# A decoder trunk whose float32 products are split in two: every fourth low part by an adding DMA

## The chip, the cores and the metric

The kernel runs on one core of one Trainium2 chip. The metric is the device time of one execution in microseconds (us); the time before is the median of two runs. A second record, the profile, comes from one further execution under the hardware profiler.

## The reference

Two decoder layers work on x, 256 tokens by 2048 features, in float32. Layer 0 mixes tokens by causal pooling (a product with `pool_w_in`, four trailing-window means, a 512 by 512 product for each of four channel groups, a product with `pool_w_out`). Layer 1 is dilated sliding-window attention with 24 heads of 128 (`attn_w_qkv` is 2048 by 9216, `attn_w_out` 1024 by 2048). After each mixer comes x = LN(alpha * x + mixer(x)), and then x = LN(alpha * x + relu(x @ w_up) ** 2 @ w_down) with 8192 hidden features. Nearly all arithmetic is products of 256 rows with large weights, each of which is read once.

## The kernel before

**Products in three terms.** TensorE gets operands of type float32r, which hold fewer bits than float32. Each float32 operand is therefore split: the high part is the value rounded to float32r, the low part is what is left. A product is summed up from high*high, low*high and high*low. For activations and weights alike, `split_from` (L61) does this: ScalarE copies the source into the high tile (L62), VectorE subtracts the high tile from the source into the low tile (L63).

**Weights in chunks.** `plan` and its helpers (L76 to L103) list all weights in the order of use as 744 chunks of 128 partitions by 1024 elements, 512 KB each: 2 blocks of 512 columns, or 4 blocks of 256. Counted from 0, chunk k passes through three steps, each with its own buffers. `load` (L108) starts a DMA on SyncE's queue into one of 4 `raw` buffers. `prefetch` (L117) splits a raw chunk into one of 8 `wh` and one of 8 `wl` buffers. TensorE then reads both. A raw buffer is free for the next load when its split is done; a `wh` or `wl` buffer is free when TensorE has done its last product with the chunk before in it.

**Order.** The instructions of TensorE, VectorE and ScalarE stay in the order in which the program writes them; the DMA queues and GpSimd are ordered by the framework's scheduler. `weights` (L128), called for each chunk in turn, first writes the splits of up to 8 chunks, the one about to be used among them, and returns that one. In the first pass over `pool_w_in` the number ahead is smaller: `min(2 + kc // 4, SPLITS)` (L183), where kc counts blocks of 128 rows, two to a chunk. `resident` (L134) takes several chunks that are used once for each of the two token tiles; the closing product of a sublayer (`closing`, L360) and the opening product of the next (`opening`, L422) work so, in order that the norm of one token tile runs beside products of the other. In `opening` only two chunks beyond the resident ones are split (L433) ahead of the second tile's products; the rest of the lookahead is written after them.

**What shares the queues with the splits.** On ScalarE: the copies of the second half of each product (L216), relu and square (L517, L519), the high parts of the activations. On VectorE: the sums and low parts that follow these, the residual sums (L277, L279, L555), the norms, and the postponed restoring of the residual (`restore`, L335), one block of 512 columns at the end of each of the next passes. On GpSimd: its few masks and counters, and the small loads of norm vectors (`gb`, L332; `last`, L512), some of which wait for a restore.

**Passes.** A pass of `feature_major` (L174) over 512 columns uses 8 chunks, each with 8 pairs of products: 512 columns with the high part (L189), 256 with the low part (L190). A pass of `token_major` (L234) uses 8 chunks too (L231).

Of the kernel before, what the change touches and what calls it, by code (L numbers as in the profile page):

```python
# [12 lines left out]
AF = mybir.ActivationFunctionType  # L13
OP = mybir.AluOpType
# [12 lines left out]
BACK = 128  # L27
# [5 lines left out]
MASKED = -1e30  # L33
CHUNK = 1024
RAWS = 4
SPLITS = 8
RESIDENT = 4
MLP_PARTS = 4
UP_FIRST = (256, 256, 512, 512, 512)
# [7 lines left out]
def trunk(ctx: ExitStack, tc: tile.TileContext, x, pool_w_in, pool_w_group, pool_scale, pool_w_out,  # L47
          attn_w_qkv, attn_w_out, mlp_w_up, mlp_w_down, ln_mix_g, ln_mix_b, ln_mlp_g, ln_mlp_b, out):
    nc = tc.nc
# [17 lines left out]

# [1 line left out]
    w_in, w_out = by_rows(pool_w_in[0]), by_rows(pool_w_out[0])  # L69
# [38 lines left out]
    def load(upto):  # L108
        """Start the loads of the chunks before `upto`."""
        while state["raw"] < min(upto, len(chunks)):  # L110
            src, step, ncols = chunks[state["raw"]]
            raw = wraw.tile([P, step, ncols], F32, tag="raw", name="raw")
            nc.sync.dma_start(raw, src)
            raws.append(raw)
            state["raw"] += 1

    def prefetch(upto):  # L117
        """Load and split the chunks before `upto`."""
        while state["split"] < min(upto, len(chunks)):
            load(state["split"] + 1)  # L120
            _, step, ncols = chunks[state["split"]]
            hi = wsplit.tile([P, step, ncols], F32R, tag="wh", name="wh")
            lo = wsplit.tile([P, step, ncols], F32R, tag="wl", name="wl")
            split_from(hi, lo, raws.pop(0))
            ready.append((hi, lo))
            state["split"] += 1

    def weights(ahead=SPLITS):  # L128
        """The next chunk, with those after it that fit into the buffers on their way."""
        prefetch(state["used"] + max(ahead, 1))  # L130
        state["used"] += 1
        return ready.pop(0)

    def resident(n):  # L134
        """The next n chunks, to be used more than once."""
        prefetch(state["used"] + n)
        state["used"] += n
        return [ready.pop(0) for _ in range(n)]

# [1 line left out]
    xz = const.tile([P, NT, D], F32, name="xz")  # L141
# [9 lines left out]

    # Per-feature vectors with the features on partitions: [128, 16] columns of each.
    rows = const.tile([7 * KT, P], F32, name="rows")
# [9 lines left out]

    # The transposed activations, the high and the low part of a block side by side.
    xT = const.tile([P, KT, 2, S], F32R, name="xT")
# [6 lines left out]

# [1 line left out]
    def feature_major(nk, ncols, act, start_up=None):  # L174
        """w.T @ act for the next pass, features on partitions: a bank for each block of 128 features,
        with the products of act's high part in its first half, those of its low part in the second."""
        nb = ncols // P
        kstep = CHUNK // ncols
        ps = [bank([P, 2, S], "pf") for _ in range(nb)]
        for kc in range(0, nk, kstep):  # L180
            if start_up is not None:
                start_up(kc)
            hi, lo = weights(SPLITS if start_up is None else min(2 + kc // 4, SPLITS))  # L183
            for j in range(kstep):
                k = kc + j
                a = act(k)
                for b in range(nb):
                    sl = slice(b * P, (b + 1) * P)
                    nc.tensor.matmul(ps[b], hi[:, j, sl], a, start=(k == 0), stop=False, skip_group_check=True)  # L189
                    nc.tensor.matmul(ps[b][:, 0, :], lo[:, j, sl], a[:, 0, :], start=False, stop=(k == nk - 1),  # L190
                                     skip_group_check=True)
        return ps

    def feature_pairs(nk, ncols, act):
        """The same with two blocks to a bank, the products of both parts of act added up."""
        nb = ncols // P
        kstep = CHUNK // ncols
        ps = [bank([P, 2, S], "pf") for _ in range(nb // 2)]
        for kc in range(0, nk, kstep):
            hi, lo = weights()  # L200
            for j in range(kstep):
                k = kc + j
                a = act(k)
                for b in range(nb):
                    sl = slice(b * P, (b + 1) * P)
                    for i, (w, part) in enumerate(((hi, 0), (hi, 1), (lo, 0))):
                        nc.tensor.matmul(ps[b // 2][:, b % 2, :], w[:, j, sl], a[:, part, :],  # L207
                                         start=(k == 0 and i == 0 and b % 2 == 0),
                                         stop=(k == nk - 1 and i == 2), skip_group_check=True)
        return ps  # L210

    def joined(out, ps):
        """The halves of each bank added up."""
        for b, p in enumerate(ps):
            low = tmp.tile([P, S], F32, tag="low", name="low")
            nc.scalar.activation(low, p[:, 1, :], AF.Copy)  # L216
            nc.vector.tensor_add(out[:, b, :], p[:, 0, :], low)  # L217
# [16 lines left out]
    def token_major(nk, ncols, act, shared=False, before_last=None):  # L234
        """Outputs [128 tokens, ncols] of both token tiles, in a bank of their own or in a shared one."""
        kstep = CHUNK // ncols
# [14 lines left out]
    def tile_products(ps, t, nk, parts, act, start=True, between=()):  # L251
        """The same for one token tile, from resident chunks."""
        k = 0
# [9 lines left out]

# [1 line left out]
    class Norm:  # L265
# [22 lines left out]
        def rstd(self, t, between=((), (), ())):  # L288
            r = self.r[t]
            nc.vector.reciprocal(r[:, 1:2], r[:, 0:1])  # L290
            self.centre(t, between[0])
            # One Newton step: r * (1.5 - 0.5 * v * r * r).
            nc.vector.tensor_scalar(r[:, 2:3], r[:, 4:5], r[:, 1:2], r[:, 1:2], op0=OP.mult, op1=OP.mult)
# [15 lines left out]
        def scaled(self, t, n):  # L309
            """Four transposed blocks, scaled and shifted per feature."""  # L310
            v = tmp.tile([P, 4, P], F32, tag="xv", name="xv", bufs=3)
# [13 lines left out]
        def restores(self):  # L325
            """The residual x = g * zhat + b, to be computed when the engines have time."""
            gbs = {}
# [32 lines left out]
    def closing(nk, act, first, norm, before_last=None):  # L360
        """The last product of a sublayer with its residual, the norm, and its transpose of token tile 0."""
        held = RESIDENT if norm.last is None else SPLITS
# [59 lines left out]
    def opening(norm, ncols):  # L422
        """The first product with the normed x, a token tile at a time, while the norm of tile 1 ends."""
        both = bank([P, NT, ncols], "pt")
# [12 lines left out]

# [1 line left out]
    def x_features(kc):  # L439
        """The blocks kc and kc + 1 of x, transposed and split."""  # L440
        pt = bank([P, 2, S], "ptr")
# [13 lines left out]
    with ExitStack() as ph:  # L455
        pool0 = ph.enter_context(tc.tile_pool(name="pool0", bufs=1))
        pbuf = ph.enter_context(tc.tile_pool(name="pbuf", bufs=2))
        # The pooled features; each group is then replaced by its product.
        pT = pool0.tile([P, KT, 2, S], F32R, name="pT")
# [46 lines left out]
    def mlp(norm_in, norm):  # L506
        with ExitStack() as ph:
# [6 lines left out]
            def hidden(ps):  # L514
                """relu(.) ** 2."""
                r = hb.tile([P, 2, S], F32, tag="r", name="r")
# [46 lines left out]

# [1 line left out]
    norm2 = Norm(ln_mix_g[1], ln_mix_b[1], 4)  # L565
    with ExitStack() as ph:
        ap1 = ph.enter_context(tc.tile_pool(name="ap1", bufs=1))
        ap = ph.enter_context(tc.tile_pool(name="ap", bufs=2))
        # dist[t][g][q, s] = s - q where query q of tile t sees key s in that group, else MASKED.
        dist = [ap1.tile([P, GROUPS, P * (t + 1)], F32, name=f"dist{t}") for t in range(NT)]  # L570
# [8 lines left out]
        def distances():  # L579
            for t in range(NT):  # L580
# [5 lines left out]
                for g, dil in enumerate(DILATIONS):  # L586
# [6 lines left out]
                    elif W > BACK:  # L593
                        # q - s <= BACK
                        nc.gpsimd.affine_select(out=dst, in_=dst, compare_op=OP.is_ge, fill=MASKED,
                                                base=BACK - t * P, pattern=[[1, W]], channel_multiplier=-1)
                    # s <= q
                    nc.gpsimd.affine_select(out=dst, in_=dst, compare_op=OP.is_ge, fill=MASKED,
# [19 lines left out]
        def scores(j, g, q, k, sc):  # L618
            """Scores of a head, biased and masked, into sc[t][:, g, :]."""
            b = j % 2  # L620
# [11 lines left out]
        def softmax(sc):  # L632
            """One softmax over the keys of all three groups."""
            ms = []
# [109 lines left out]
```

## Time and profile before

| what | value |
|---|---|
| median of 2 runs | 2161.73 us (2161.68 to 2161.79) |
| span of the profiled execution, first to last instruction | 2159.9 us |
| TensorE matmul busy | 2141.0 us, 99% |
| VectorE busy | 1284.2 us, 59% |
| ScalarE busy | 1058.4 us, 49% |
| GpSimd busy | 23.0 us, 1% |
| DMA | 404.69 MB, mean 187 GB/s |

The profiled execution has no time of its own beside its span; the median of the runs is 1.8 us above that span, which is what lies around the first and last instruction. Busy times of different engines overlap; the share that matters is that of the engine on which the end waits. The granted TensorE clock is full over nearly the whole span (mean 0.998).

### The profile page before, as it was taken

How to read it: one execution, taken by the hardware profiler on the slowest of the kernel's cores; microseconds unless marked ns; L12 is line 12 of the kernel's file. 1: busy time of each engine (PE TensorE's matmuls, PEld its weight loads, DVE VectorE, ACT ScalarE, POOL GpSimd, SP SyncE). 2: the span in 40 equal slices, each digit the busy share in tenths (PEclk: the TensorE clock that was granted, in tenths of full speed). 3: DMA queues.
4: the chain of work that ended last, by engine and by line, in shares of the span. 5: the costliest groups of instructions: out<-in, count | busy, mean ns of one | idle time of the engine just before them, and what ended most of it. 6: DMA issues, size and time to landing. Idle time of an engine off the chain costs nothing.

```text
span 2159.9 us, 30318 instructions
## 1 busy us (share of the span) xinstructions
PE 2141.0 (99%) x12033; PEld 1867.7 (86%) x12033; DVE 1284.2 (59%) x1558; ACT 1058.4 (49%) x1368; POOL 23.0 (1%) x52
## 2 busy tenths in 40 slices
PE   8999999999999999999999999999999999999998
PEld 7889888888888888898999898988888888888887
DVE  6785756555455555578656565676655555554555
ACT  4463654454355355354545444455545534644541
POOL 1000000000000000001000000000000000000000
PEclk9999999999999999999999999999999999999999
DMA  7565567665655655548554555456675565565552
GB/s 240 201 213 177 176 195 237 176 201 194 190 181 195 195 174 198 194 139 232 175 176 156 176 159 173 160 167 214 204 223 177 199 195 186 176 205 185 182 201 95
DMA packets 255662, 404.69 MB, mean 187 GB/s; under 512 B 12720, under 2 KB 109600, under 8 KB 255264
## 3 DMA queue, kind: packets, MB, share of 16 engines
q1 hardware_dynamic: 253088, 394.31, 55.9%
q0 software_dynamic: 2432, 8.45, 1.9%
q8 instruction: 94, 1.54, 0.3%
q14 instruction: 48, 0.39, 0.1%
HBM read 400.61 MB, written 2.10 MB: 186 GB/s over the span
## 4 chain that ended last, share of the span: by engine, by line
PE 97%; DVE 2%; DMA 1%; ACT 0%; issue 0%; SPq 0%; DVEq 0%; ACTq 0%
PE pt L231 45%; PE pf L189 32%; PE pf L190 16%; PE pf L207 1%; PE po L665 1%; PE pq L626 1%; DMA raw<-in_attn_w_qkv 0%; DVE wl L63 0%; PE ptr L307 0%; DMA raw<-in_pool_w_in 0%; ACT xv L316 0%; ACT wh L62 0%; DVE xT L323 0%; DVE xT L322 0%; DVE xz L349 0%
## 5 line engine op out<-in xcount | busy, mean ns | idle before, releaser
L63 DVE TENSOR_TENSOR wl<-raw,wh 128x1024 fp32r<-128x1024 f32 x744 | 898.4, 1224 | 643.3 <-ACT wh L62 638.9
L62 ACT ACTIVATE wh<-raw 128x1024 fp32r<-128x1024 f32 x744 | 775.9, 1058 | 823.1 <-PE pt L231 362.9
L189 PE MATMUL pf<-xT,wh 128*128 128x512 f32 x3008 | 1066.2, 399 | 0.0
L190 PE MATMUL pf<-xT,wl 128*128 128x256 f32 x3008 | 845.2, 281 | 0.3 <-DVE wl L63 0.3
L189 PEld LDWEIGHTS pf<-xT,wh 128*128 128x128 f32 x3008 | 566.1, 188 | 139.5
L190 PEld LDWEIGHTS pf<-xT,wl 128*128 128x128 f32 x3008 | 568.9, 189 | 1.1 <-DVE wl L63 0.8
L231 PE MATMUL pt<-wh,hH 128*128 128x512 f32 (+1 forms) x1088 | 406.7, 377 | 0.0
L231 PE MATMUL pt<-wl,hH 128*128 128x512 f32 (+1 forms) x1088 | 406.6, 377 | 0.0
L231 PE MATMUL pt<-wh,hL 128*128 128x512 f32 (+1 forms) x1088 | 397.9, 377 | 0.0
L231 PEld LDWEIGHTS pt<-wh,hH 128*128 128x128 f32 x1088 | 204.8, 188 | 37.6
L231 PEld LDWEIGHTS pt<-wl,hH 128*128 128x128 f32 x1088 | 204.8, 188 | 37.3
L231 PEld LDWEIGHTS pt<-wh,hL 128*128 128x128 f32 x1088 | 199.6, 188 | 37.4
L231 PE MATMUL pt<-wh,xT 128*128 128x256 f32 x896 | 167.0, 285 | 1.9 <-DVE xT L322 1.5
L231 PEld LDWEIGHTS pt<-wh,xT 128*128 128x128 f32 x896 | 141.4, 192 | 3.3 <-DVE xT L322 3.1
L231 PE MATMUL pt<-wl,xT 128*128 128x256 f32 x448 | 123.6, 283 | 0.0
L63 DVE TENSOR_TENSOR hL<-q,hH 128x512 fp32r<-128x512 f32 x62 | 42.9, 693 | 125.6 <-ACT hH L62 125.6
L216 ACT ACTIVATE low<-pf 128x256 f32<-128x256 f32 x188 | 64.7, 379 | 56.1 <-PE pf L190 49.1
L231 PEld LDWEIGHTS pt<-wl,xT 128*128 128x128 f32 x448 | 85.9, 192 | 0.0
L231 PE MATMUL pt<-wh,pT 128*128 128x512 f32 (+1 forms) x320 | 82.6, 347 | 0.0
L217 DVE TENSOR_TENSOR u<-pf,low 128x256 f32<-128x256 f32 x172 | 65.6, 420 | 13.0 <-ACT low L216 13.0
L517 ACT ACTIVATE r<-u 128x512 f32<-128x512 f32 x62 | 39.2, 632 | 49.6 <-DVE u L217 49.6
L231 PEld LDWEIGHTS pt<-wh,pT 128*128 128x128 f32 x320 | 56.1, 189 | 7.5
(126 smaller groups left out, 1000.8 us busy)
## 6 DMA issues: line engine op xcount, KB each, us to landing
raw<-in_mlp_w_up SPq DMA_DIRECT2D x256, 512.0 KB, 4.2
raw<-in_mlp_w_down SPq DMA_DIRECT2D x256, 512.0 KB, 4.2
raw<-in_attn_w_qkv SPq DMA_DIRECT2D x144, 512.0 KB, 3.8
raw<-in_pool_w_in SPq DMA_DIRECT2D x32, 512.0 KB, 5.2
raw<-in_pool_w_out SPq DMA_DIRECT2D x32, 512.0 KB, 4.5
raw<-in_attn_w_out SPq DMA_DIRECT2D x16, 512.0 KB, 4.0
raw<-in_pool_w_group SPq DMA_DIRECT2D x8, 512.0 KB, 4.9
gb<-in_ln_mix_g POOLq DMA_DIRECT2D x8, 256.0 KB, 4.3
```

Source lines behind the costliest of these rows:

```text
L62: nc.scalar.activation(hi, src, AF.Copy)
L63: nc.vector.tensor_sub(lo, src, hi.bitcast(F32))
L189: nc.tensor.matmul(ps[b], hi[:, j, sl], a, start=(k == 0), stop=False, skip_group_check=True)
L190: nc.tensor.matmul(ps[b][:, 0, :], lo[:, j, sl], a[:, 0, :], start=False, stop=(k == nk - 1), skip_group_check=True)
L207: nc.tensor.matmul(ps[b // 2][:, b % 2, :], w[:, j, sl], a[:, part, :], start=(k == 0 and i == 0 and b % 2 == 0), stop=(k == nk - 1 and i ...
L216: nc.scalar.activation(low, p[:, 1, :], AF.Copy)
L217: nc.vector.tensor_add(out[:, b, :], p[:, 0, :], low)
L231: nc.tensor.matmul(ps, a[:, sl], u, start=(start and k == 0 and i == 0), stop=(k == nk - 1 and i == 2), skip_group_check=True)
L517: nc.scalar.activation(r, ps, AF.Relu)
L626: nc.tensor.matmul(pq[:, t, :], q[u][:, b, sl], k[v][:, b, :], start=(i == 0), stop=(i == 2))
L665: nc.tensor.matmul(po, v[:, st, b * P:(b + 1) * P], p[:, g, sl], start=(i == 0), stop=(i == 3 * 2 * GROUPS - 1))
```

## The change

For the chunks 3, 7, 11 and so on, 186 of the 744, the split is made otherwise. ScalarE first writes the negated rounded raw chunk into the low tile, then GpSimd's queue issues a DMA that reads the same 512 KB of weights from HBM once more and adds them onto the low tile, and ScalarE makes a second pass over the raw chunk for the high tile. VectorE does not touch these chunks. The other chunks are split as before. Comments are also taken out, which changes no instruction.

```diff
+ADDED = 4
...
     def prefetch(upto):
         while state["split"] < min(upto, len(chunks)):
             load(state["split"] + 1)
             _, step, ncols = chunks[state["split"]]
             hi = wsplit.tile([P, step, ncols], F32R, tag="wh", name="wh")
             lo = wsplit.tile([P, step, ncols], F32R, tag="wl", name="wl")
-            split_from(hi, lo, raws.pop(0))
+            raw = raws.pop(0)
+            if state["split"] % ADDED == ADDED - 1:
+                nc.scalar.activation(lo, raw, AF.Copy, scale=-1.0)
+                nc.gpsimd.dma_start(lo, chunks[state["split"]][0], accum_op=OP.add)
+                nc.scalar.activation(hi, raw, AF.Copy)
+            else:
+                split_from(hi, lo, raw)
             ready.append((hi, lo))
             state["split"] += 1
```

## Rows read from the trace of the kernel before

**Rows 1.** The page: busy us (share of the span) and instructions of each engine.
```profile
PE 2141.0 (99%) x12033; PEld 1867.7 (86%) x12033; DVE 1284.2 (59%) x1558; ACT 1058.4 (49%) x1368; POOL 23.0 (1%) x52
```

**Rows 2.** The page's chain that ended last, by engine.
```profile
PE 97%; DVE 2%; DMA 1%; ACT 0%; issue 0%; SPq 0%; DVEq 0%; ACTq 0%
```

**Rows 3.** Waits of TensorE's products: line, releaser, us in total, times, longest.
```profile
PE ptr L444 <- DMA xz<-in_x: 5.8, 2, 3.2
PE pt L231 <- DVE xT L322: 1.5, 3, 1.0
PE pf L190 <- DVE wl L63: 0.3, 1, 0.3
PE pq L626 <- DVE qkL L63: 0.2, 1, 0.2
```

**Rows 4.** The page's groups of the weights' splits: count, busy us, mean ns, idle before.
```profile
L63 DVE TENSOR_TENSOR wl<-raw,wh 128x1024 fp32r<-128x1024 f32 x744 | 898.4, 1224 | 643.3 <-ACT wh L62 638.9
L62 ACT ACTIVATE wh<-raw 128x1024 fp32r<-128x1024 f32 x744 | 775.9, 1058 | 823.1 <-PE pt L231 362.9
```

**Rows 5.** Added chunks: split on ACT, first low product on PE (start, us).
```profile
17.83 1.05 ACT L62 ACTIVATE wh<-raw 128x1024 fp32r<-128x1024 f32 x1
20.32 0.48 PE L189 MATMUL pf<-xT,wh 128*128 128x512 f32 x1
20.63 0.28 PE L190 MATMUL pf<-xT,wl 128*128 128x256 f32 x1
...
118.98 1.04 ACT L62 ACTIVATE wh<-raw 128x1024 fp32r<-128x1024 f32 x1
124.17 0.28 PE L207 MATMUL pf<-pT,wl 128*128 128x256 f32 x1
...
609.44 1.06 ACT L62 ACTIVATE wh<-raw 128x1024 fp32r<-128x1024 f32 x1 [2.01 <-DMA raw<-in_mlp_w_up]
629.14 0.28 PE L190 MATMUL pf<-xT,wl 128*128 128x256 f32 x1
...
1542.27 1.04 ACT L62 ACTIVATE wh<-raw 128x1024 fp32r<-128x1024 f32 x1
1547.58 0.39 PE L231 MATMUL pt<-wl,hH 128*128 128x512 f32 x1
```

**Rows 6.** DMA issues: KB each, median us from issue to landing.
```profile
raw<-in_mlp_w_up SPq DMA_DIRECT2D x256, 512.0 KB, 4.2
gb<-in_ln_mix_g POOLq DMA_DIRECT2D x8, 256.0 KB, 4.3
gb<-in_ln_mix_b POOLq DMA_DIRECT2D x8, 256.0 KB, 6.1
```

**Rows 7.** DMA queues: packets, MB, share of 16 engines' span.
```profile
q1 hardware_dynamic: 253088, 394.31, 55.9%
q0 software_dynamic: 2432, 8.45, 1.9%
q8 instruction: 94, 1.54, 0.3%
q14 instruction: 48, 0.39, 0.1%
```

**Rows 8.** Stretches: PE, PEld, DVE, ACT, POOL busy (instructions), clock, DMA share, GB/s.
```profile
0.00:20.00 20.00, 13.86 (x65) 11.16 (x66) 7.57 (x9) 8.51 (x10) 5.54 (x17) 1.00 0.90 312
311.00:398.00 87.00, 87.00 (x386) 72.06 (x385) 52.97 (x53) 42.76 (x47) 1.06 (x2) 1.00 0.70 231
488.50:575.50 87.00, 87.00 (x386) 72.03 (x385) 45.09 (x43) 37.94 (x41) 0.00 (x0) 1.00 0.60 193
...
2100.00:2160.00 60.00, 49.31 (x308) 44.58 (x307) 34.33 (x55) 11.38 (x13) 0.00 (x0) 0.94 0.30 105
```

**Rows 9.** A pass's end: GpSimd's `gb` loads; VectorE's restore and subtractions; ScalarE's next chunk.
```profile
327.43 0.54 POOL L332 DMA_DIRECT2D gb<-in_ln_mlp_g  x1 [23.26 <-DVE xz L339]
...
326.45 0.69 DVE L339 TENSOR_TENSOR xz<-xz,gb 128x512 f32<-128x512 f32 x1
327.06 4.62 DVE L63 TENSOR_TENSOR wl<-raw,wh 128x1024 fp32r<-128x1024 f32 x4
...
323.66 3.89 ACT L62 ACTIVATE wh<-raw 128x1024 fp32r<-128x1024 f32 x4
335.78 1.06 ACT L62 ACTIVATE wh<-raw 128x1024 fp32r<-128x1024 f32 x1 [8.23 <-DMA raw<-in_mlp_w_down]
```

## The prediction

> **What bounds the kernel now.** I read the busy shares first: matmuls fill 2141.0 of 2159.9 us, VectorE, whose work the change takes, 59% [rows 1]. The chain that ended last says the same, 97% TensorE [rows 2]. TensorE's waits then show what could be won: products wait 7.8 us in all, of which the weights' subtraction causes 0.3 us, once [rows 3]. Of the 18.9 us in which TensorE is not busy, 6.1 lie in the first 20 us and 10.7 in the last 60 [rows 8], before its first products and after its last. So VectorE is not late, and nothing that relieves it can shorten the kernel by more than these few us: even all 18.9 us would be 0.9%.
>
> The question is then only whether a changed chunk comes too late. I asked the trace, for every fourth chunk, how long after the end of ScalarE's pass TensorE starts its first product with the low part, counting products in program order to know the chunk. I call this the gap. In the regular stretches it is long: chunk 219 is done at 610.5 and first used at 629.1, a gap of 18.6 us [rows 5]. The median over the 186 is 18.0 us. It is short where the splits were written late: in the first pass, where few chunks are ahead, after an opening, and at pass ends where ScalarE first does the activations. Eleven of the 186 are under 6 us: chunk 3 with 1.7, 23 with 5.3, 31 with 4.8, 39 with 4.2, 43 with 5.8, 79 with 5.3, 111 with 5.2, 115 with 4.0, 495 with 5.4, 523 with 5.6 and 527 with 4.3 (the first, one between and the last in [rows 5]; for chunk 39, 118.98 + 1.04 = 120.02 to 124.17). Five more lie between 6 and 7, sixteen between 7 and 10.
>
> **The change, part by part.** *VectorE* loses 186 subtractions of 1224 ns, 227.7 us [rows 4]. TensorE waited 0.3 us for them, so this is worth 0. There is one indirect gain: at a pass end VectorE does the restore first, and the subtractions of a group of four run from 327.06 to 331.68; until then the raw buffers are held, and ScalarE gets its next chunk, 115, at 335.78 after 8.23 us of waiting for a load [rows 9]. Chunk 111, the first of that group, is now freed by ScalarE at about 325.8 instead of after the first subtraction at about 328.3, so the load of 115 starts some 2.5 us sooner and its gap grows from 4.0 to 6.5. Chunks 523 and 531, which follow 519 and 527 in the same way, gain as much.
>
> *ScalarE* gets 186 more passes of 1058 ns, 196.8 us [rows 4], 49% becoming 58%. The negation takes the place of the old pass in its queue; the high pass and all behind it come 1.06 us later, once in four chunks. The cover is the same gap: the high part of chunk 3 is used 0.3 us ahead of the low one [rows 5], and no changed chunk has less than 1.7 us. Other chunks behind it lose 1.06 us to ScalarE and win 1.22 us from VectorE. I cost it at 0; without cover it would be 1 us at the places where ScalarE goes chunk after chunk, some ten of them, so up to 10 us.
>
> *SyncE's queue* issues the same 744 loads; a raw buffer of a changed chunk now waits for two ScalarE passes (2.1 us) instead of a pass and a subtraction (2.3 us). 0.
>
> *GpSimd* gets 186 issues of about 0.54 us [rows 9], 100 us on an engine with 23 us of work [rows 1]. Its queue is in order: an adding DMA can stand behind a `gb` load that waits for a restore. In the one pass end shown that load came at 327.43, 2.7 us after chunk 111's negation would end (324.7). I take 0, since the scheduler may place the adding DMA first; the bound is 2.7 us at some ten restores, hence 27 us at most and less where the gap is wide.
>
> *The adding DMA* decides. From the negation's end it must land within the gap, or TensorE stands still, and everything after shifts. Its price is in no row. Nearest rows: a 512 KB load on SyncE's queue lands 4.2 us after issue; the 256 KB loads on GpSimd's queue 4.3 us, or 6.1 us as the second of two [rows 6]. It moves twice the bytes of the latter and must also read what it adds onto. GpSimd's queue used 1.9% of 2159.9 us for 8.45 MB [rows 7], so 0.5243 MB at that pace take 1.9% x 2159.9 x 0.5243 / 8.45 = 2.5 us on all 16 engines; 0.25 MB take half, 1.3 us. From 4.3 us follow 3.0 us that do not depend on the size, so 5.5 us if the reading back is free and 8.1 us if it doubles the transfer. I take 7 us, between them. The lower end is 4.3 us. As the upper end I take 10 us: 8.1 plus 2 us of queueing behind raw loads, about the difference between 6.1 and 4.3.
>
> The Trainium skill, "Collectives: The Full Stack", Part 3 (the bandwidth ceiling), says that a reduce-scatter runs at about half the rate of an all-gather since each of its adding transfers reads two sources, and that the addition itself costs nothing. By that rule the landing is the 8.1 us end, and the sum below would be some 38 us, 2200 us; no run here shows an addition yet, so I leave it as one end.
>
> Sum at 7 us, over the gaps under 7: 5.3 + 1.7 + 2.2 + 2.8 + 1.2 + 1.7 + 1.8 + 1.6 + 2.7 for chunks 3, 23, 31, 39, 43, 79, 111, 495 and 527, which is 21.0; 115, 523 and 531 drop out by the earlier load; four more between 6 and 7 (chunks 7, 107, 335, 519) give 1.7. That is 23 us, of which a part may be shared, as a stall also gives later chunks time. Against the profiled execution 2159.9 + 23 = 2183 us; the median of the runs is 1.8 us above that span, so **2185 us**, 1.1% slower. At 4.3 us only chunk 3 and traces of two others are left, 3 us: 2165 us. At 8 us the same sum is 45 less 8 for the three eased chunks, 37 us: 2199 us. At 10 us the 32 gaps under 10 give 95 less 14, 81 us: 2243 us. A loss of 2% (43 us) is reached at about 8.3 us.
>
> **Does TensorE slow down beside more DMA?** No: two equal stretches of 87 us hold 386 products each, with DMA at 231 and at 193 GB/s [rows 8]. 0.
>
> **Rivals.** *The adding DMA lands later than 8.3 us.* For it: it reads two sources, and the DMA engines are 0.90 busy in the first 20 us and 0.70 in the stretch that holds chunks 111 and 115 [rows 8], just where gaps are short. Against it: most raw loads land in 4.2 us under the same load. 2205 to 2260 us, 2243 in the middle; place: the thin gaps after start-up and the openings.
>
> *The DMA engines become the bound.* They are busy 55.9 + 1.9 + 0.4 = 58% [rows 7]. The 186 transfers carry 97.5 MB: 13.8% at the pace of the raw loads, 27.6% with the reading back at that pace, 21.9% at GpSimd's pace, 43.9% with both [rows 7]. So 72 to 102%, which holds, barely at the top: 2205 us at 102%. If an adding byte costs three times the GpSimd pace, it is 124% and 2680 us. The point is 42% of the span, 4.9 us of all 16 engines for each transfer. It would show in the whole span, not in thin gaps.
>
> *It is hidden.* At a landing of 5 us or less the loss is 7 us or less, 2162 to 2169 us.
>
> *Faster by 2%* would need 43 us from a TensorE that idles 18.9.
>
> **How the numbers follow.** My forecast, a loss of 7 to 43 us, gets 0.44; hidden 0.15; late landing 0.25; DMA-bound 0.15; faster 0.01. The measurement can tell 2%, some 43 us, from no change. Same is 0.44 + 0.15 = 0.59, slower 0.25 + 0.15 = 0.40. The range runs from 2162 (hidden) to 2260 (10 us landing, and some of GpSimd's queueing); it leaves out most of the DMA-bound case and the edges, under 2 in 10.
>
> **What would show it.** In the changed profile: median landing of the adding DMAs on GpSimd's queue (7 us; over 8.3 the late rival), new waits of TensorE's low products for that DMA, a score of them and some 20 us in total, the longest at chunk 3 with about 5 us; VectorE down by 228 us, ScalarE up by 197; DMA share between 72 and 102%. Waits spread evenly over all passes would make the reasoning wrong, and so would a TensorE that runs slower without waiting.

## The result: 2.8% slower, by waits and by what follows a wait

The changed kernel takes 2222.65 us (median; 2220.44 to 2224.87), a ratio of 1.028 to the kernel before, with an interval of 1.026 to 1.0299. The forecast was 2185 us. The profiled execution took 2220.44 us, its span is 2218.7 us, 58.8 us more than before. Lines of the changed part are now L128 (negation), L129 (adding DMA), L130 (high part); L63 and L64 are the two halves of the old split, and every later line moves by 8 (in the kernels of the experiments by some more).

The page of the changed kernel: busy us and instructions of each engine, the chain that ended last, the two DMA queues that matter (packets, MB, share of 16 engines), three DMA issues (KB each, median us to landing), and GpSimd's issues of adding DMAs (busy us, mean ns).

```profile
PE 2158.6 (97%) x12033; PEld 1879.1 (85%) x12033; DVE 1061.8 (48%) x1372; ACT 1227.4 (55%) x1554; POOL 251.4 (11%) x238
...
q1 hardware_dynamic: 253088, 394.31, 54.1%
q0 software_dynamic: 65056, 105.98, 26.2%
...
PE 84%; issue 8%; DMA 6%; DVE 1%; ACT 1%; POOL 0%; DVEq 0%; POOLq 0%; ACTq 0%
...
L129 POOL DMA_DIRECT2D wl<-in_mlp_w_up x64 | 77.2, 1206 | 699.8 <-ACT wl L128 614.9
...
raw<-in_mlp_w_up SPq DMA_DIRECT2D x256, 512.0 KB, 5.5
...
wl<-in_mlp_w_up POOLq DMA_DIRECT2D x64, 512.0 KB, 8.8
wl<-in_mlp_w_down POOLq DMA_DIRECT2D x64, 512.0 KB, 9.0
```

Against [rows 1], VectorE lost 222 us and ScalarE won 169 (228 and 197 were foreseen), and neither is near the bound. The line to look at is the first: the same 12033 products keep TensorE busy 17.6 us longer. The chain, 97% TensorE in [rows 2], now has 6% DMA in it. The raw loads, 4.2 us in [rows 6], land in 5.5 us, and an adding DMA in 8.8 to 9.0 us.

TensorE's waits in the changed kernel: line, releaser, us in total, times, longest.

```profile
PE pf L198 <- DMA wl<-in_pool_w_in: 13.3, 4, 7.2
PE pt L239 <- DMA wl<-in_mlp_w_down: 10.9, 5, 3.7
PE pf L198 <- DMA wl<-in_mlp_w_up: 10.0, 3, 5.4
PE ptr L452 <- DMA xz<-in_x: 5.5, 3, 3.2
PE pf L198 <- DMA wl<-in_attn_w_qkv: 4.7, 1, 4.7
PE pf L215 <- DMA wl<-in_pool_w_group: 2.9, 1, 2.9
PE pt L239 <- DVE xT L330: 1.5, 3, 1.0
```

Five of these seven lines are new against [rows 3]: 14 waits for an adding DMA, 41.8 us. They stand at chunks 3, 7, 15, 31, 39, 79, 111, 175, 239, 303, 335, 495 and 527, and one of 0.2 us at 519: in the first passes, behind openings and at pass ends. TensorE's idle time grew from 18.9 to 60.1 us, by 41.2. With the 17.6 us of busier TensorE that is 58.8 us, the whole difference of the spans.

The second part is seen around one wait. First the steps of chunk 495 in the changed kernel (start, us): ScalarE's negation, GpSimd's issue, TensorE's first low product.

```profile
1496.06 1.04 ACT L128 ACTIVATE wl<-raw 128x1024 fp32r<-128x1024 f32 x1
...
1497.40 1.31 POOL L129 DMA_DIRECT2D wl<-in_mlp_w_up  x1 [17.59 <-ACT wl L128]
...
1507.99 0.58 PE L198 MATMUL pf<-xT,wl 128*128 128x256 f32 x1 [5.38 <-DMA wl<-in_mlp_w_up]
```

From the end of the negation (1497.10) to the product are 10.9 us, where the gap was 5.4. Now the same stretch by windows: busy us (instructions) of PE, PEld, DVE, ACT, POOL, then the granted clock, the DMA share, GB/s.

```profile
1496.00:1502.00 6.00, 6.00 (x36) 5.20 (x35) 3.62 (x3) 4.06 (x5) 1.31 (x1) 1.00 0.88 275
1502.00:1506.60 4.60, 0.62 (x4) 0.25 (x2) 1.23 (x1) 3.06 (x3) 1.19 (x1) 1.00 1.15 261
1506.60:1513.40 6.80, 5.41 (x18) 4.73 (x19) 3.67 (x3) 3.18 (x3) 0.00 (x0) 0.50 1.08 326
1513.40:1520.00 6.60, 6.60 (x40) 5.81 (x39) 3.49 (x7) 5.25 (x9) 0.96 (x1) 1.00 0.57 219
```

TensorE stood still from 1502.6 to 1508.0. From 1506.6 on, still within the wait, the granted clock is 0.50 (1.2 GHz) for 6.8 us: 18 products in 5.4 busy us, where the last window has 40 in 6.6. The mean granted clock fell from 0.998 to 0.989. Eight stretches at 0.50 stand at waits in the changed kernel, five of 6.8 us and three of 3.4 (chunks 7, 15 and 111); the six waits at 31, 39, 175, 239, 303 and 519, of 0.2 to 2.9 us, have none. Before there was one such stretch, at the very end.

### The profile page after: what moved, and what is told of

It reads as the page before. It is cut to its first block, busy times and chain, and to the rows that moved or that the text cites. A ratio compares the mean times of both kernels' runs of the same rounds, so it can differ in the third digit from the quotient of the medians.

```text
span 2218.7 us, 30635 instructions
## 1 busy us (share of the span) xinstructions
PE 2158.6 (97%) x12033; PEld 1879.1 (85%) x12033; DVE 1061.8 (48%) x1372; ACT 1227.4 (55%) x1554; POOL 251.4 (11%) x238
## 3 DMA queue, kind: packets, MB, share of 16 engines
q1 hardware_dynamic: 253088, 394.31, 54.1%
q0 software_dynamic: 65056, 105.98, 26.2%
## 4 chain that ended last, share of the span: by engine, by line
PE 84%; issue 8%; DMA 6%; DVE 1%; ACT 1%; POOL 0%; DVEq 0%; POOLq 0%; ACTq 0%
PE pt L239 39%; PE pf L197 28%; PE pf L198 14%; DMA wl<-in_mlp_w_down 2%; DMA wl<-in_mlp_w_up 2%; DMA wl<-in_pool_w_in 1%; PE po L673 1%; PE pf L215 1%; PE pq L634 1%; DMA wl<-in_attn_w_qkv 0%; DMA wl<-in_pool_w_group 0%; DMA raw<-in_mlp_w_down 0%; DMA rows<-in_ln_mix_b 0%; PE ptr L315 0%; ACT wl L128 0%
## 5 line engine op out<-in xcount | busy, mean ns | idle before, releaser
L64 DVE TENSOR_TENSOR wl<-raw,wh 128x1024 fp32r<-128x1024 f32 x558 | 673.9, 1224 | 899.8 <-ACT wh L63 881.9
L63 ACT ACTIVATE wh<-raw 128x1024 fp32r<-128x1024 f32 x558 | 580.3, 1056 | 499.3 <-PE pt L239 183.6
L239 PE MATMUL pt<-wl,hH 128*128 128x512 f32 (+1 forms) x1088 | 409.0, 379 | 10.9 <-DMA wl<-in_mlp_w_down 10.9
L128 ACT ACTIVATE wl<-raw 128x1024 fp32r<-128x1024 f32 x186 | 196.4, 1056 | 213.5 <-DMA raw<-in_mlp_w_down 91.6
L130 ACT ACTIVATE wh<-raw 128x1024 fp32r<-128x1024 f32 x186 | 194.2, 1044 | 0.0
L129 POOL DMA_DIRECT2D wl<-in_mlp_w_up x64 | 77.2, 1206 | 699.8 <-ACT wl L128 614.9
L129 POOL DMA_DIRECT2D wl<-in_mlp_w_down x64 | 77.2, 1207 | 566.0 <-ACT wl L128 558.9
L64 DVE TENSOR_TENSOR hL<-q,hH 128x512 fp32r<-128x512 f32 x62 | 42.9, 692 | 125.7 <-ACT hH L63 125.7
L129 POOL DMA_DIRECT2D wl<-in_attn_w_qkv x36 | 46.4, 1289 | 387.6 <-ACT wl L128 288.6
```

The source lines that it names most:

```text
L63: nc.scalar.activation(hi, src, AF.Copy)
L64: nc.vector.tensor_sub(lo, src, hi.bitcast(F32))
L128: nc.scalar.activation(lo, raw, AF.Copy, scale=-1.0)
L129: nc.gpsimd.dma_start(lo, chunks[state["split"]][0], accum_op=OP.add)
L130: nc.scalar.activation(hi, raw, AF.Copy)
L239: nc.tensor.matmul(ps, a[:, sl], u, start=(start and k == 0 and i == 0), stop=(k == nk - 1 and i == 2), skip_group_check=True)
```

## The experiments

**What is free: the second ScalarE pass.** The adding DMA alone is left out.

```diff
                 nc.scalar.activation(lo, raw, AF.Copy, scale=-1.0)
-                nc.gpsimd.dma_start(lo, chunks[state["split"]][0], accum_op=OP.add)
                 nc.scalar.activation(hi, raw, AF.Copy)
```

> The changed kernel without the adding DMA: ScalarE still writes the negated chunk and the high tile, TensorE multiplies with the negated chunk as it stands (the addition of the raw weights is left out). If the loss is the landing of the adding DMA, TensorE waits for none of these chunks, its clock stays full, and the time is 2158 to 2166 us, as before. If the loss is ScalarE's second pass over every fourth chunk, it stays above 2200 us.

Measured: 2162.22 us, ratio 1.0002 (0.9993 to 1.0012). So the extra ScalarE work costs nothing, and taking 222 us off VectorE gives nothing. All of the loss comes with the adding DMA.

**What is free: adding DMAs where the gap is long.** 41 changed chunks (start-up, pass ends, openings) go back to VectorE; 145 stay with the adding DMA.

```diff
...
-            if state["split"] % ADDED == ADDED - 1:
+            if state["split"] % ADDED == ADDED - 1 and state["split"] not in THIN:
```

> The adding DMA only where the gap is long: of the 186 chunks, the 41 whose gap was under about 12 us, or at which TensorE waited, are split by VectorE as before; 145 keep the adding DMA. Theory A: neither waits nor a lower clock are left, 2159 to 2168 us. Theory B, raw loads slowed by the other adding DMAs still cost: above 2180 us.

Measured: 2161.71 us, 0.9999 (0.9989 to 1.0008). Two lines of this kernel's page:

```profile
PE 2140.5 (99%) x12033; PEld 1867.5 (86%) x12033; DVE 1110.1 (51%) x1413; ACT 1188.8 (55%) x1513; POOL 200.9 (9%) x197
...
wl<-in_mlp_w_up POOLq DMA_DIRECT2D x50, 512.0 KB, 8.8
```

And all waits of its TensorE:

```profile
PE ptr L453 <- DMA xz<-in_x: 6.0, 2, 3.3
PE pt L240 <- DVE xT L331: 1.5, 3, 1.0
PE pf L199 <- DVE wl L65: 0.3, 1, 0.3
```

The landing is as slow as before, 8.8 us, yet no product waits for it and TensorE is not busier. So the DMA engines as a whole are not the bound, and TensorE does not slow down beside the traffic as such. Only the places where the gap is short (thin) cost.

**The price of adding.** A plain copy of the same bytes on the same queue takes the place of the addition (the low tile then holds the whole weight).

```diff
-                nc.gpsimd.dma_start(lo, chunks[state["split"]][0], accum_op=OP.add)
+                nc.gpsimd.dma_start(lo, chunks[state["split"]][0])
```

> The changed kernel with a plain copy of the weights in place of the addition, on the same queue, onto the same tile, behind the same negation (the subtraction is left out). If reading the destination back doubles the transfer, its packets take half the time (0.09 to 0.1 us for 2 KB in place of 0.18), it lands some 2 to 3 us earlier, about 6 to 6.5 us after issue, and by the gaps of the kernel before the loss is 15 to 20 us of waits and less than 8 of clock: 2175 to 2190 us. If the price is that of any DMA from GpSimd's queue, nothing changes: 2215 us and more.

Measured: 2183.92 us, 1.0099 (1.0084 to 1.0114), within the first forecast. The copy lands sooner, and its queue has a smaller share:

```profile
q0 software_dynamic: 65056, 105.98, 19.4%
...
wl<-in_mlp_w_up POOLq DMA_DIRECT2D x64, 512.0 KB, 6.6
wl<-in_mlp_w_down POOLq DMA_DIRECT2D x64, 512.0 KB, 7.1
```

The 7 us that I took is thus what a plain copy takes here; adding costs 2 us more (3.4 for `attn_w_qkv`, 7.9 against 4.5), and waits fall to 16.6 us without it. Where the 2 us go is seen in the packets in which a DMA moves its bytes. At 88 chunks no other DMA of GpSimd's queue was on its way in either kernel. There the first packet starts 3.9 us (median) after the start of the issue with the addition and 1.5 us without it; from the first packet to the landing it takes 4.3 and 5.0 us. So what adding costs here passes before the first packet, 0.5 us of it in the longer issue (1.21 us against 0.71).

The Trainium skill, "Collectives: The Full Stack", Part 3, says that the adding transfers of a reduce-scatter run at about half rate since they read two sources. The trace agrees in direction and not in size: less the 1.9% of other loads, the adding DMAs take 24.3% and the copies 17.5%, 1.4 times as much.

**Four chunks alone.** The adding DMA only at chunks 3, 79, 335 and 495.

```diff
+FOUR = (3, 79, 335, 495)
...
-            if state["split"] % ADDED == ADDED - 1:
+            if state["split"] in FOUR:
```

> The adding DMA at four chunks alone, 3, 79, 335 and 495, where the changed kernel waited 7.2, 4.4, 4.7 and 5.4 us with no further wait near; all others are split by VectorE as before. Theory: each costs its wait, somewhat shorter for want of other adding DMAs (18 us in all), and behind each the granted clock falls to its lower level and costs 2 to 3 us more (8 to 10 us): 2186 to 2191 us. Rival, the clock costs nothing of its own: 2178 to 2181 us.

Measured: 2190.78 us, 1.0135 (1.012 to 1.015), as expected. From its page, the engines' busy times:

```profile
PE 2148.0 (98%) x12033; PEld 1873.5 (86%) x12033; DVE 1280.1 (58%) x1554; ACT 1063.4 (49%) x1372; POOL 28.5 (1%) x56
```

Its TensorE's waits for these DMAs:

```profile
PE pf L199 <- DMA wl<-in_mlp_w_up: 10.3, 2, 5.4
PE pf L199 <- DMA wl<-in_pool_w_in: 7.3, 1, 7.3
...
PE pf L199 <- DMA wl<-in_attn_w_qkv: 4.5, 1, 4.5
```

Four transfers among 744 loads cost 29 us: 22.1 of waits and 7.0 of busier TensorE. From the negation's end to the product they take 9.2, 10.4, 10.7 and 10.9 us, no less than in the full change (9.1, 9.9, 10.8, 10.9). So here the late landing is the price of one adding DMA beside raw loads, and not of a jam of adding DMAs.

**Pass ends alone.** The same edit with chunks 111, 175, 239, 303 and 527.

> Adding DMAs at the pass-end chunks 111, 175, 239, 303 and 527 alone; all others split as before. In the changed kernel these wait 3.6, 1.6, 1.0, 1.1 and 3.7 us. Theory, the gap there was shortened by the adding DMAs of their neighbours, which make raw loads and so ScalarE's pass late: without the neighbours 175, 239 and 303 do not wait at all (gaps of 12.6 us against a landing of 8 to 10), and only 111 and 527 do, by 8 to 10 less their gaps of 5.2 and 4.3, 3 to 5 us each and up to 2 us of clock each: 2168 to 2174 us. Rival, these chunks' own landing is longer there: all five wait as in the changed kernel, 11 us and the clock behind five waits: 2176 to 2182 us.

Measured: 2174.31 us, 1.0054 (1.0041 to 1.0066), 0.3 us above what the theory gave and below the rival. All waits for the adding DMAs:

```profile
PE pt L240 <- DMA wl<-in_mlp_w_down: 8.3, 2, 4.4
```

And the steps of chunk 175 (start, us): TensorE begins chunk 167, ScalarE negates, GpSimd issues, TensorE takes the first low product.

```profile
491.85 0.40 PE L198 MATMUL pf<-xT,wh 128*128 128x512 f32 x1
...
500.29 1.04 ACT L129 ACTIVATE wl<-raw 128x1024 fp32r<-128x1024 f32 x1
...
501.63 1.23 POOL L130 DMA_DIRECT2D wl<-in_mlp_w_down  x1 [171.53 <-ACT wl L129]
...
513.97 0.39 PE L240 MATMUL pt<-wl,hH 128*128 128x512 f32 x1
```

Only 111 and 527 wait; 175, 239 and 303 have a gap of 12.6 us, as before, and no wait. The same chunk in the changed kernel, with ScalarE's passes ahead of it:

```profile
518.64 1.06 ACT L63 ACTIVATE wh<-raw 128x1024 fp32r<-128x1024 f32 x1 [3.07 <-DMA raw<-in_mlp_w_down]
518.77 0.40 PE L197 MATMUL pf<-xT,wh 128*128 128x512 f32 x1
...
523.74 1.06 ACT L63 ACTIVATE wh<-raw 128x1024 fp32r<-128x1024 f32 x1 [2.69 <-DMA raw<-in_mlp_w_down]
532.01 1.04 ACT L128 ACTIVATE wl<-raw 128x1024 fp32r<-128x1024 f32 x1
...
542.60 0.50 PE L239 MATMUL pt<-wl,hH 128*128 128x512 f32 x1 [1.55 <-DMA wl<-in_mlp_w_down]
```

There the negation begins 13.2 us after chunk 167, not 8.4: ScalarE waited for raw loads that came late beside the adding DMAs of neighbouring chunks. The gap shrinks to 8.0 us, and the landing, 9.5 us after the negation here and 8.8 with these five alone, no longer fits. The Trainium skill, "DMA: Bandwidth & Descriptors", section "Issuing engines are not separate DMA queues", says that transfers of all issuers share the 16 engines. The raw loads agree: they land in 5.5 us with 186 adding DMAs and in 4.2 us with these five.

**Little traffic, same lateness.** Two adding DMAs of 64 KB one after the other, 24.4 MB instead of 97.5; most of the addition is left out.

```diff
-                nc.gpsimd.dma_start(lo, chunks[state["split"]][0], accum_op=OP.add)
+                src = chunks[state["split"]][0]
+                for _ in range(2):
+                    nc.gpsimd.dma_start(lo[:, 0:1, 0:128], src[:, 0:1, 0:128], accum_op=OP.add)
```

> The landing without the traffic: in place of 512 KB, two adding DMAs of 64 KB (512 bytes a partition) onto the same part of the low tile, the second behind the landing of the first, so that the low tile is ready some 9 us after the negation as in the changed kernel, with a quarter of its bytes (most of the addition is left out). Theory A, the late landing is the loss: 2205 to 2225 us. Theory B, the traffic beside the raw loads is the loss: 2162 to 2180 us. Both: between them.

Measured: 2204.85 us, 1.0201 (1.0184 to 1.0218), at the lower edge of Theory A and 18 us under the full change. The lateness with a quarter of the bytes thus makes 43 of the 61 us.

```profile
raw<-in_mlp_w_up SPq DMA_DIRECT2D x256, 512.0 KB, 4.4
...
wl<-in_mlp_w_up POOLq DMA_DIRECT2D x128, 64.0 KB, 4.6
```

At chunks 3, 79, 335 and 495 the products come 9.4, 10.2, 10.3 and 9.5 us after the negation and wait 7.4, 4.8, 4.1 and 4.0 us, nearly as in the full change. At 175, 239, 303 and 527 they do not wait, and at 111 only 0.4 us: raw loads land in 4.4 us, and the gaps are longer (12.6 us at 175, 239 and 303). A small adding DMA lands in 4.6 us, so of the 8.8 us about half does not depend on the size.

**What follows a wait.** Products of a zero operand, added to sums that they do not change, fill the wait, so that TensorE does not stand still. First at all thin chunks of the changed kernel:

```diff
+FILL = {3: 30, 7: 11, 15: 11, 31: 3, 39: 12, 79: 19, 111: 15, 175: 6, 239: 4, 303: 4, 335: 20, 495: 23, 527: 16}
...
+    def fill(ps, w, ncols, k):
+        for _ in range(FILL.pop(k, 0) * 512 // ncols):
+            nc.tensor.matmul(ps, w, zero.to_broadcast([P, ncols]), start=False, stop=False, skip_group_check=True)
...
```

> The changed kernel with products of zero columns added into the accumulating bank ahead of the first low product of the 13 chunks for which TensorE waited over 0.8 us, about 90% of each wait filled. The end of each wait does not move. Theory: the 17.6 us by which TensorE's busy time grew come from the lower granted clock that follows the waits; with TensorE active through them the clock stays at its full level and the time falls by 14 to 20 us, to 2202 to 2209 us. Rival, the clock falls for another reason: 2220 us or, where products of zeros outlast a wait, more.

Measured: 2224.45 us, 1.0283 (1.0266 to 1.03): a miss, no gain. Its waits for the adding DMAs:

```profile
PE pf L209 <- DMA wl<-in_mlp_w_up: 10.5, 3, 5.5
...
PE pf L209 <- DMA wl<-in_pool_w_in: 4.5, 5, 1.4
PE pt L252 <- DMA wl<-in_mlp_w_down: 2.1, 2, 1.2
...
PE pf L209 <- DMA wl<-in_attn_w_qkv: 1.2, 1, 1.2
```

TensorE's time without the 40.2 us of zero products is 2145.9 us instead of 2158.6, so most of the clock came back, 12.7 us. But 18.3 us of waits and 40.2 of zero products take 16.7 us more than the 41.8 us of waits before: a new wait of 5.5 us stands at chunk 103 and one of 3.8 at 519. TensorE came to chunk 103 some 1.8 us sooner than in the changed kernel, and its negation, after ScalarE had waited 1.46 and 1.79 us for raw loads, ended 3.4 us later (330.4 against 326.9). Then at the four isolated chunks, where no thin neighbour follows:

```diff
+FILL = {3: 24, 79: 12, 335: 10, 495: 13}
+FOUR = (3, 79, 335, 495)
...
```

> The same four adding DMAs, with products of zero columns added into the accumulating bank through most of each wait (5.2, 2.6, 2.2 and 2.8 us). The end of each wait stays where it is. Theory: TensorE is active, its clock stays full, and only the waits are left: 8 to 10 us faster than the run without the filling, 2178 to 2182 us. Rival, the clock costs nothing of its own or falls all the same: no difference between the two.

Measured: 2188.72 us, 1.013 (1.0113 to 1.0147), a miss too, not to be told from the 2190.78 without filling. The filling was too short: 2.2 to 2.7 us were left at each chunk, and at each rest 3.4 us at the lower clock came again.

```profile
PE pf L210 <- DMA wl<-in_mlp_w_up: 4.8, 2, 2.6
PE pf L210 <- DMA wl<-in_pool_w_in: 2.7, 1, 2.7
PE pf L210 <- DMA wl<-in_attn_w_qkv: 2.2, 1, 2.2
```

So once more, long enough:

```diff
-FILL = {3: 24, 79: 12, 335: 10, 495: 13}
+FILL = {3: 38, 79: 23, 335: 21, 495: 26}
```

> Adding DMAs at chunks 3, 79, 335 and 495 alone, as in the run that did only these (2190.8 us, 22 us of waits in four places, matmuls 7.0 us longer), but with enough zero products to fill the whole of each wait (38, 23, 21 and 26 of 512 columns at some 0.225 us), where the earlier filled run left 2 to 3 us of each. Theory, the granted clock falls because TensorE stood still, and that is a cost of its own behind each wait: no wait over 0.5 us at the four places, the clock at full level up to the end, matmuls less the zero products 2141 us, and so 2161.7 + 22 for the landing + 1 to 2 of zero products too many = 2184 to 2186 us. Rival, the loss behind a wait comes from the supply of the next chunks and the clock only shows it: 2189 to 2191 us, as without the filling.

Measured: 2186.45 us, 1.0116 (1.0101 to 1.0132), 0.5 us above the theory's range and 2.5 below the rival's. Its page:

```profile
PE 2164.5 (99%) x12141; PEld 1887.8 (86%) x12141; DVE 1280.1 (59%) x1555; ACT 1062.9 (49%) x1372; POOL 28.5 (1%) x56
```

What is left of its waits for the adding DMAs:

```profile
PE pf L210 <- DMA wl<-in_mlp_w_up: 0.7, 1, 0.7
PE pf L210 <- DMA wl<-in_attn_w_qkv: 0.3, 1, 0.3
```

By windows (length, PE busy and count, other engines where they are shown, clock, DMA share, GB/s): the zero products alone over the whole span, and all work in the stretch of chunk 495.

```profile
0.00:2185.40 2185.40, 24.25 (x108) 1.00 0.58 186
...
1477.00:1483.00 6.00, 6.00 (x31) 5.23 (x29) 2.79 (x3) 2.44 (x3) 0.00 (x0) 1.00 1.12 300
1483.00:1490.00 7.00, 7.00 (x43) 6.14 (x42) 4.88 (x6) 5.14 (x8) 0.00 (x0) 1.00 0.90 317
```

With TensorE busy the clock stays at 1.00 through the same lateness, and 2164.5 - 24.25 = 2140.3 us remain for the products, as before the change (2141.0). The spans say 2185.4 against 2189.1 without filling; the intervals of the ratios overlap, so that this costs TensorE time is shown by the busy time and the clock, and its size in the end only roughly, some 4 us of 29.

**Experiments that were confounded.** To have the full traffic without the wait, TensorE's low products of changed chunks read the high tile instead (numbers change):

```diff
-            ready.append((hi, lo))
+            ready.append((hi, hi if state["split"] % ADDED == ADDED - 1 else lo))
```

> The changed kernel with all its instructions and DMAs, but for the changed chunks TensorE's low products read the high tile, so that no product waits for an adding DMA (the low part of these chunks is left out of the result). Theory: only the wait for the landing costs, hence 2160 to 2168 us although the DMA engines carry the same 98 MB more. Rival, the DMA engines or SBUF are contended and slow the raw loads or TensorE itself: above 2200 us.

Measured: 2225.8 us, 1.0295 (1.0279 to 1.031). The unread low tile comes free at once, and VectorE, the next writer, waits for the adding DMA to land (some 340 us in all), which makes its splits late. To mend that, the low tile was read once, by the last low product of the chunk that follows:

```diff
+        if state["used"] % ADDED == 0:
+            state["fresh"] = lo
+            return hi, hi
...
+                    if j == kstep - 1 and b == nb - 1:
+                        u = tail(u)
...
```

> All instructions and DMAs of the changed kernel, but TensorE reads the low tile of a changed chunk only once, in the last low product of the next chunk, up to 5.6 us later; its other low products read the high tile (the low part is left out of the result). The low tile is so held as long as before or a little longer, and no other engine gets it while the DMA runs. Theory A, TensorE's wait for the landing is the whole loss: 2160 to 2172 us. Theory B, part of the loss is that the raw loads of all chunks land later beside the adding DMAs (5.5 us in place of 4.2): 2180 to 2205 us.

Measured: 2191.42 us, 1.0136 (1.012 to 1.0151). Here the held tile delays ScalarE's negations (they wait some 290 us for products), and products still wait some 13 us for adding DMAs. Neither run isolates the traffic.

**High products first** in the changed chunks, so that the low part is needed some us later; sums are taken in another order.

```diff
...
+            if late:
+                for p in pairs:
+                    high(*p)
+            for p in pairs:
+                if not late:
+                    high(*p)
+                low(*p)
...
```

> The changed kernel, but in a changed chunk TensorE does all products with the high part first, in the passes with features on partitions and in the passes with tokens on partitions outside of the resident chunks. The first low product comes some 1.7 us later in the former (8 products of 0.21 us), some 3.4 us in the latter. Of the 41.9 us of waits in the changed kernel about 19 should be left (chunk 3 from 7.2 to 5.5, 79 from 4.4 to 2.7, 495 from 5.4 to 3.7, those in the passes with tokens on partitions near 0). With the clock loss shrinking along, 2185 to 2195 us; if the lower clock is not tied to the waits, about 2200 us; if the wait is not for the low part, 2222 us.

Measured: 2210.58 us, 1.0225 (1.0209 to 1.024), a miss. Waits of the isolated chunks shrank (7.2 to 5.3 at chunk 3, 4.4 to 2.7 at 79), others came up (5.3 us at 103, 2.2 at 519), and 39.7 us of waits for adding DMAs remained. As in the first filled run, time won at one thin chunk is partly waited for at the next.

## Why the prediction was wrong

**What held.** TensorE bounds the kernel, VectorE's relief is worth 0 (the run without the adding DMA), ScalarE's second pass costs 0 by itself, the loss sits in thin gaps (the run that spares them loses nothing), and the longest wait is at chunk 3. The DMA-bound rival, 54.1 + 26.2 = 80% busy, did not come true. GpSimd's queue cost nothing: at all 14 chunks that waited, the issue comes 0.3 to 0.4 us after the negation. The rival *lands later than 8.3 us* came true, and with two costs that it did not have.

**The first step that failed: the landing of 7 us.** From the negation's end it took 8.3 to 10.9 us at the chunks that waited; from issue, the median is 8.8 to 9.0 us for the MLP's weights. The pace came from the 256 KB `gb` loads, and I set 7 us between a free and a doubled reading back. The plain copy already takes 6.6 to 7.1 us, and the addition's price passes ahead of the first packet (3.9 us against 1.5), not in a doubled transfer; the issue takes 1.21 us of GpSimd, not 0.54. At chunks 3, 7, 15, 79, 111, 335 and 495 the gap, read without the wait, stayed within 0.3 us of the gap before, so there the landing alone makes the wait: 30.5 us where the sum at 7 us had 11.5. It is not simply the sum at a later landing: at 8 us that gave 37, at 10 us 81. Chunks 23 and 43, with gaps under 6 us, do not wait at all: their gaps are 8.8 and 10.0 us, since a wait shortly before gives them time. In the run with the plain copy, where 7, 15, 31 and 39 do not wait, 23 and 43 do (2.7 and 1.9 us). Chunk 115's gap grows from 4.0 to 11.2 us already in the run without the adding DMA: the earlier load that the prediction foresaw (to 6.5 us), and more.

**The second step: gaps taken as fixed.** ScalarE and SyncE stood at 0 because their own work was covered. But the gap hangs on the raw load, and the adding DMAs make raw loads later by 1.3 us each. At chunks 175, 239 and 303 the gap shrinks from 12.6 us to 8.0, 9.0 and 9.0, and the landing comes 9.5 to 10.1 us after the negation where alone it came after 8.7 to 8.8; together that makes waits, 3.7 us in all. By the start of every twelfth chunk, in program order, the changed kernel loses 4.5 us there.

**The third step: nothing was priced behind a wait.** The prediction asked whether TensorE slows down *beside* more DMA, found 0, and was right. It did not ask what comes *after* TensorE stood still: 17.6 us of longer products at the lower clock. The row for it was there, the clock of 0.94 in the last 60 us of [rows 8], where TensorE is idle for 10.7. By the sum, with the waits alone the time would have been 2159.9 + 41.2 + 1.8 = 2203 us, 1.9% slower, and the clock carries it over 2%; no run shows the waits of the full change without the clock.

The places add up. By the delay of each chunk's first product the four chunks alone cost 29.2 us and the pass ends alone 12.8. The changed kernel loses 12.5 us more than the first of these up to chunk 48 (22.2 against 9.7; chunks 7, 15, 31 and 39 wait there) and 4.5 at 175, 239 and 303: 29.2 + 12.8 + 12.5 + 4.5 = 59.0 against 58.8 measured. The last two terms are read from the changed kernel itself, so the sum shows only that the six chunks that wait in the two small runs cost together what they cost in the full change. It is not a proof that the parts don't touch one another; the filled run shows that they do.

**What stays open.** How much of the 17.6 us is a loss of its own: filled in the full change it gave nothing, at four isolated chunks some 4 us of 7. And why an adding DMA alone among raw loads takes 10.4 to 10.9 us at chunks 79, 335 and 495 but 8.6 to 8.7 at 111 and 527. The traces point at the raw loads: while the transfer was on its way the DMA engines were 1.00 to 1.01 busy, at 254 to 276 GB/s, at the first three, and 0.74 to 0.75 busy, at 165 to 170 GB/s, at the other two. The first three also have blocks of 256 columns instead of 512, but the adding DMAs of `attn_w_qkv`, with blocks of 256 too, landed in 7.9 us (median). No run varied the raw loads alone. No version beats the kernel before; sparing the thin chunks equals it.

## What to carry to other kernels

Where work moves from an engine that is not the bound to a longer path, look for the thinnest gaps, not at busy shares: 41 of 186 chunks held the whole loss. Price the new transfer with everything from the releasing instruction to the waiting one, and then ask what it does to the loads that set the gap itself. And add, to each wait of TensorE, the time at the lower clock behind it: here 1.3 to 1.8 us a wait on the mean (17.6 us over 14 waits, six of them without any; 7.0 over 4).

## What the runs showed of the hardware

An adding DMA of 512 KB on GpSimd's queue landed in 7.9 to 9.0 us (medians by weight) where a plain copy took 4.5 to 7.2, and a raw load on SyncE's queue 5.3 to 6.9 beside it; of 64 KB, in 4.6 us (`mlp_w_up`). Its issue kept GpSimd 1.21 us (`mlp_w_up`), against 0.58 for a `gb` load in the same kernel. Its first packet started 3.9 us after the start of the issue, that of the plain copy 1.5 us (medians of the same 88 chunks).

At a wait of 5.4 us the granted clock fell to 1.2 GHz 1.4 us before the wait ended and stayed there for 6.8 us; at rests of 2.2 to 2.7 us it was there for 3.4 us; with products on zeros in place of the waits it stayed at 2.4 GHz. A product of 256 columns with the low part had a median of 415 ns at the lower level and 281 ns at the higher one.
